# One more pair of projections by seven half products, another order of the projections, and a third row turn laid out by transfers

## The chip, the cores and the metric

The kernel runs on one core of one Trainium2 chip. The metric is the device time of one execution in microseconds (us), median of three runs. The core has a matrix engine (TensorE, PE in the profile; its weight loads are PEld), three engines that work elementwise (VectorE, DVE; ScalarE, ACT; GpSimd, POOL), a queue that issues transfers (SyncE, SP), and 16 DMA engines. Each engine runs its own instructions in order; semaphores tie them together.

## The reference

One encoder layer for 512 tokens of width 1024, all in float32: two attention mixers beside each other (A: windowed, 16 query heads and 4 key heads; B: three groups of four heads with window and dilation (128,1), (512,4), (2048,16)), merged by sigmoid gates, then an output projection, a layer norm, a SwiGLU of width 2816 and a second layer norm.

```python
proj = h @ w_in[l]
qa, ka, va, qb, kb, vb = jnp.split(proj, SPLITS, axis=-1)
qa = rope_partial(qa.reshape(b, s, A_Q_HEADS, HEAD_DIM), pos)
...
o_a = windowed_gqa_sink(qa, ka, va, a_sink[l]).astype(h.dtype)
o_b = dilated_mixture(qb, kb, vb).astype(h.dtype)
gates = jax.nn.sigmoid(h @ w_gate[l] + b_gate[l])
g_a, g_b = jnp.split(gates, N_BRANCH, axis=-1)
mixed = g_a * (o_a @ w_br_a[l]) + g_b * (o_b @ w_br_b[l])
y = mixed @ w_out[l]
h = layer_norm(DN_ALPHA * h + y, ln1_g[l], ln1_b[l])
f = (jax.nn.silu(h @ w_ff_gate[l]) * (h @ w_ff_up[l])) @ w_ff_down[l]
h = layer_norm(DN_ALPHA * h + f, ln2_g[l], ln2_b[l])
```

The rotation (rope) touches the first 16 of the 64 dimensions of a head: it mixes two blocks of eight rows with cosines and sines.

## The kernel before

**Precision.** Every float32 factor is split into a high part (rounded to the engine's fast format, a copy on ScalarE or VectorE, line 387 or 389) and a low part (the rest, a subtraction on VectorE, line 558 or 413). A product is three matmuls: high by high, high by low, low by high.

**Single projections.** 128 output features over 512 tokens are eight blocks of three matmuls of 512 columns (feat_k, lines 537 to 539), 24 matmuls into one bank of PSUM. The weights come as two halves of 256 KB (half_unit), each split once.

**Pairs by seven half products.** pair_x takes two projections at once by the scheme of Strassen and Winograd: a 2 x 2 block product by seven products instead of eight. Each is 12 matmuls of 256 columns (lines 659 to 661). It needs sums of the weight halves: S1 and S3 are loaded with a second transfer that adds in flight (load_sum, issued by POOL at line 401), S2 and S4 are added on VectorE, or for a pair of the kind "D:" by further adding transfers (line 624). All seven factors are split. The token side needs shifted forms of x, made once by x_forms (step X in the order). ScalarE evacuates partial results (keep, line 667), VectorE combines them (lines 680 and 682). A pair holds two banks, y and xz.

**Rotation.** A single q or k is rotated out of its bank (rotate, lines 772 to 778, two VectorE operations that read the bank and two that do not). Results of pairs are rotated in turns of several tiles (turn_rows): transfers gather the 16 rotated rows of each head into one tile G; a second tile H has the same rows with the two blocks of eight exchanged. In the form R, H is made from G by a stream shuffle on VectorE (line 746). In the form r, H is laid out by transfers alone, four more of 16 KB for each tile, straight from the source (line 742). Then follow two products, a sum, and transfers back (line 754).

**Order.** Every operation has a priority: the planned TensorE time T at which its step stands in the list ORDER, plus an offset of the step (the number behind @) and one of its kind (FORMS, EV and others). A greedy planner at build time (Program.run) goes through time with estimated durations, gives each free engine the ready operation of lowest priority whose buffers fit, and so fixes the order of each engine's queue. On the chip every queue is followed in that order. Buffers are slots of SBUF and eight banks of PSUM, handed out first in, first out (b.room, line 274); at most three banks serve the projections (class dense). SPARE slots are kept free for the oldest waiting buffer.

**ORDER's words.** P: and D: are pairs; q, k, Q, K with digits are projections of mixers A and B; VA, V0, V12 are values; g is a gate; A and B are attention units; O fetches an attention output of A from memory (fetch_oa, allowed after the unit that OA_AFTER names); R and r are row turns over everything that waits for one. Two gates are computed along with the first projections k0, q0 and VA; their results and those of the other gates of B are put away in memory and fetched back. Branches (lines 1487 to 1507) multiply the attention outputs by w_br_a and w_br_b and apply the gates; the output projection (tok_major), the norm and the SwiGLU (also by seven half products, lines 1759 to 1761) follow. In ORDER before, 13 pairs stand; the single gates g stand around B2 and behind B3; X stands first; k0 and q0 are rotated right behind the first projections, outside the list (line 1332).

Of the kernel before, what the change touches and what calls it, by code (L numbers as in the profile page):

```python
# [15 lines left out]
P = 128  # L16
S = 512
D = 1024
# [31 lines left out]
SAME = {PE: 0.0, ACT: 0.1, DVE: 0.1, POOL: 0.1}  # L50
HOLD = 0.25
BIAS = 0.2
SPARE, SPARE2 = (4, 12)
ROOMS = {2: dict(whl=16), 3: dict(whl=20, ws=8)}


# [28 lines left out]


ORDER = """
X@-11 VA@-23 q2@-799 q1@-877 P:q3,g@-124 R@-106 D:k1,q4@-31 R@155 P:q5,Q01@-843 A0@-168 D:q6,q7@-47 D:g,g@-34 r@631 P:g,Q00@-22 L@-4 A2@-96
D:g,K00@-31 A1@-48 R@187 V12@-20 P:g,K01@-67 R@-5 P:Q02,K02@-28 A3@-55 V0@55 R@5 B0@-7 B1@11 O@25 O@35 P:K10,Q10@-39 O@-13 O@-54 K11@-34 R@24
O@11 P:Q12,Q11@-30 g@28 K12@-12 O@950 g@25 r O@43 P:g,g@-2 B2@-525 O@-304 B3@21 g@-29 P:g,g@-32 g@-8  # L90
"""
FORMS = -255.0
VAL = 140.0
OA_AFTER = (1, 0, 0, 0, 0, 1, 0, 0)
XT_AFTER, LN_AFTER = [('B', 2), ('B', 2), ('B', 2), ('B', 2)], "b4"
STORE, OA, OA_SPLIT, OB_SPLIT, N_OA, N_XA = 0.0, -60.0, -140.0, -140.0, 4, 4
PACK = -60.0
# [40 lines left out]
class Program:  # L138


    def __init__(self, limits):
        self.limits = limits
        self.used = {k: 0 for k in limits}
        self.ops = []
        self.writer, self.readers = {}, {}
        self.T = 0.0
        self.spare = SPARE
        self.strict = self.hold = False
        self.rooms = {}

    @staticmethod
    def buf_of(tok):
# [2 lines left out]
    def op(self, alts, fn, reads=(), writes=(), prio=0.0, after=(), abs_prio=None, moves=0.0, extra=0, table=None):  # L155
        o = Op()
# [19 lines left out]
        for t in list(reads) + list(writes):  # L176
            b = self.buf_of(t)
# [6 lines left out]
            d.succ.append(o)  # L184
        self.ops.append(o)
        return o

    def fits(self, o):
        need = {}
# [17 lines left out]
    def run(self):  # L207
        engines = (PE, ACT, DVE, POOL, SP)
        free = dict(START)
# [25 lines left out]
        while n_left:  # L235
# [5 lines left out]
            while frees and frees[0][0] <= now:  # L241
                _, _, b = heapq.heappop(frees)
# [6 lines left out]
            while progress:  # L249
                progress = False  # L250
                for e in engines:
# [13 lines left out]
                    o = best  # L265
# [5 lines left out]
                    for b in o.bufs:  # L271
                        if b.tile is None:
                            if b.keys[0] in self.rooms:
                                b.room = self.rooms[b.keys[0]].popleft()
                                b.tile = b.make(b.room)
                            else:
                                b.tile = b.make()
                            for key in b.keys:
                                if key in self.limits:
                                    self.used[key] += 1  # L280
# [64 lines left out]
def hybrid_layer(ctx: ExitStack, tc: tile.TileContext, wpack, xT, xtok, sink, bgate,  # L345
# [20 lines left out]
    def slot(dt=F32, cls=None):  # L366
        cls = cls or "gen"
        return Buf("slot", cls, lambda r: slab.tile([P, S], dt, tag=f"slab{r}", bufs=1, name=name("sl")))

    def bank(cls):  # L370
        return Buf("bank", cls, lambda r: psum.tile([P, S], F32, tag=f"bank{r}", bufs=1, name=name("ps")))
# [85 lines left out]
    def unit(u):  # L457
        return [half_unit(u, 0), half_unit(u, 1)]
# [37 lines left out]
    for j in range(KD):  # L496
# [3 lines left out]
        for c0, c1 in ((0, S // 2), (S // 2, S)) if j == 0 else ((0, S),):  # L500
            w, sk = c1 - c0, (st, c0)
# [45 lines left out]
    def feat_x(ps, wu):  # L547
        for k in range(KD):
            feat_k(ps, wu, k, XM, xtok_of)
# [206 lines left out]
                   reads=gs, writes=[(R, "r", h)], prio=EV)  # L756
            op([(POOL, 0.0)], lambda e: None, reads=[(R, "r", 0), (R, "r", 1)], writes=[R], prio=EV)

    def in_sbuf(u):

        ps, t = bank("dense"), slot()
        feat_x(ps, unit(u))
        op([(ACT, act(S, True))], lambda e: copy(ACT, halves(t.t), back(ps.t)), reads=[ps], writes=[(t, 1), (t, 2)], prio=EV)
        return t

# [551 lines left out]
    psk, psq, psv = bank("dense"), bank("dense"), bank("dense")  # L1317
# [11 lines left out]
    op([(POOL, 0.0)], lambda e: pr.limits.update(whl=N_WHLA, ws=N_WSA), after=[pr.ops[-1]])  # L1329
    for f in range(N_ALONG):  # L1330
        gate(8 + f, ps=along[f])
    ka, qa = {0: k_near(psk, 4)}, {0: q_near(psq, 4, (0, 0))}
    load(mB, maskb, prio=0)
    env = {"gate": N_ALONG, "turn": [], "qs": {}, "ks": {}}

# [57 lines left out]
    def step(w):  # L1393
        if w == "X":
            x_forms()
        elif w == "L":
            op([(POOL, 0.0)], lambda e: pr.limits.update(ws=N_WS, whl=N_WHL), after=[env["mark"]])
        elif w[:2] in ("P:", "D:"):
# [26 lines left out]
        elif w[0] == "A":  # L1425
            g = int(w[1])
# [688 lines left out]
```

## Time and profile before

| | |
|---|---|
| median of three runs | 724.7 us (724.18 to 724.98) |
| the profiled execution | 724.82 us, its span 723.0 us |
| mean granted TensorE clock | 0.998 |
| POOL busy | 173.2 us (24% of the span) |
| instructions | 14810 |
| memory read by transfers | 119.69 MB |
| transfers of 16 KB between tiles (SP) | 28 |
| stream shuffles in row turns (line 746) | 6 |

The span goes from the first to the last instruction on the core; the time of an execution has about 1.8 us around it. Where the prediction shows groups of instructions, each row has the line of the kernel, engine, operation, tiles and shapes, then a count, busy time, the mean ns of one, and the idle time of the engine ahead of them with what ended it. Matmuls overlap: their durations are longer than the distance between their starts.

### The profile page before, as it was taken

How to read it: one execution, taken by the hardware profiler on the slowest of the kernel's cores; microseconds unless marked ns; L12 is line 12 of the kernel's file. 1: busy time of each engine (PE TensorE's matmuls, PEld its weight loads, DVE VectorE, ACT ScalarE, POOL GpSimd, SP SyncE). 2: the span in 40 equal slices, each digit the busy share in tenths (PEclk: the TensorE clock that was granted, in tenths of full speed). 3: DMA queues.
4: the chain of work that ended last, by engine and by line, in shares of the span. 5: the costliest groups of instructions: out<-in, count | busy, mean ns of one | idle time of the engine just before them, and what ended most of it. 6: DMA issues, size and time to landing. Idle time of an engine off the chain costs nothing.

```text
span 723.0 us, 14810 instructions
## 1 busy us (share of the span) xinstructions
PE 712.5 (99%) x4947; PEld 667.2 (92%) x4947; DVE 664.4 (92%) x1425; ACT 494.6 (68%) x1136; POOL 173.2 (24%) x347
## 2 busy tenths in 40 slices
PE   8999999999999999999999999999999999999996
PEld 6889999998999998988888999999999999999985
DVE  6998999999999989999958998999999999999987
ACT  5768889889878997767625666756567566666821
POOL 0113343322423591550020022121121201212000
PEclk9999999999999999999999999999999999999999
DMA  8978967887568789766690499776897868979402
GB/s 257 294 215 210 235 168 213 227 216 179 137 169 204 187 255 253 219 196 219 199 210 33 110 300 232 177 203 165 238 238 197 223 164 219 253 196 194 106 29 88
DMA packets 81275, 141.44 MB, mean 196 GB/s; under 512 B 11024, under 2 KB 15760, under 8 KB 81200
## 3 DMA queue, kind: packets, MB, share of 16 engines
q1 hardware_dynamic: 63472, 107.07, 46.3%
q0 software_dynamic: 17456, 33.30, 26.6%
q8 instruction: 39, 0.64, 0.4%
q14 instruction: 36, 0.29, 0.1%
q10 hardware_dynamic: 272, 0.13, 0.1%
HBM read 119.69 MB, written 8.39 MB: 177 GB/s over the span
## 4 chain that ended last, share of the span: by engine, by line
PE 90%; DMA 4%; DVE 3%; SPq 2%; ACT 1%; issue 0%; POOL 0%; DVEq 0%; ACTq 0%; POOLq 0%
PE ps L1761 10%; PE ps L1759 10%; PE ps L1760 9%; PE ps L659 5%; PE ps L661 5%; PE ps L660 5%; PE ps L537 4%; PE ps L538 4%; PE ps L539 4%; PE ps L1970 4%; PE ps L1972 4%; PE ps L1971 4%; PE ps L1018 3%; DMA sl<-wpack 3%; PE ps L1549 3%; PE ps L1551 3%
## 5 line engine op out<-in xcount | busy, mean ns | idle before, releaser
L387 ACT ACTIVATE sl<-sl 128x512 fp32r<-128x512 f32 (+3 forms) x457 | 253.8, 588 | 60.7 <-DVE sl L558 43.3
L558 DVE TENSOR_TENSOR sl<-sl,sl 128x512 fp32r<-128x512 f32 (+3 forms) x415 | 245.3, 628 | 6.0 <-ACT sl L387 5.0
L387 ACT ACTIVATE sl<-ps 128x256 f32<-128x256 f32 (+6 forms) x214 | 88.5, 440 | 76.6 <-PE ps L1761 53.0
L401 POOL DMA_DIRECT2D sl<-wpack x70 | 63.0, 931 | 319.1 <-DMA sl<-wpack 92.0
L1760 PE MATMUL ps<-sl,sl 128*128 128x256 f32 x352 | 96.8, 275 | 0.0
L1761 PE MATMUL ps<-sl,sl 128*128 128x256 f32 x352 | 96.8, 275 | 0.0
L1759 PE MATMUL ps<-sl,sl 128*128 128x256 f32 x352 | 96.8, 275 | 0.0
L1759 PE MATMUL ps<-x,sl 128*128 128x256 f32 x264 | 72.6, 275 | 0.0
L1760 PE MATMUL ps<-x,sl 128*128 128x256 f32 x264 | 72.6, 275 | 0.0
L1761 PE MATMUL ps<-x,sl 128*128 128x256 f32 x264 | 72.6, 275 | 0.0
L1759 PEld LDWEIGHTS ps<-sl,sl 128*128 128x128 f32 x352 | 67.6, 192 | 0.1
L1760 PEld LDWEIGHTS ps<-sl,sl 128*128 128x128 f32 x352 | 67.6, 192 | 0.1
L1761 PEld LDWEIGHTS ps<-sl,sl 128*128 128x128 f32 x352 | 67.6, 192 | 0.0
L537 PE MATMUL ps<-x,sl 128*128 128x512 f32 (+1 forms) x161 | 62.1, 386 | 0.7 <-ACT x L387 0.7
L539 PE MATMUL ps<-x,sl 128*128 128x512 f32 (+1 forms) x161 | 60.9, 378 | 0.0
L659 PE MATMUL ps<-sl,sl 128*128 128x256 f32 x208 | 57.8, 278 | 0.9 <-ACT sl L667 0.9
L661 PE MATMUL ps<-sl,sl 128*128 128x256 f32 x208 | 57.3, 276 | 0.0
L660 PE MATMUL ps<-sl,sl 128*128 128x256 f32 x208 | 57.2, 275 | 0.0
L558 DVE TENSOR_TENSOR sl<-sl,ps 128x512 f32<-128x512 f32 (+1 forms) x72 | 47.3, 661 | 9.0 <-PE ps L1972 5.8
L1759 PEld LDWEIGHTS ps<-x,sl 128*128 128x128 f32 x264 | 50.6, 192 | 0.4
L1760 PEld LDWEIGHTS ps<-x,sl 128*128 128x128 f32 x264 | 50.6, 192 | 0.4
L1761 PEld LDWEIGHTS ps<-x,sl 128*128 128x128 f32 x264 | 50.7, 192 | 0.0
(174 smaller groups left out, 2006.6 us busy)
## 6 DMA issues: line engine op xcount, KB each, us to landing
sl<-wpack SPq DMA_DIRECT2D x254, 256.0 KB
sl<-wpack POOLq DMA_DIRECT2D x70, 256.0 KB, 5.5
wf<-wpack SPq DMA_DIRECT2D x51, 256.0 KB
sl<-sl SPq DMA_DIRECT2D x56, 128.0 KB
wf<-wpack POOLq DMA_DIRECT2D x24, 256.0 KB, 5.3
oa<-sl POOLq DMA_DIRECT2D x32, 128.0 KB, 3.6
sl<-sl SPq DMA_DIRECT2D x72, 32.0 KB
gz<-sl SPq DMA_DIRECT2D x8, 256.0 KB
```

Of the source, the lines that this page charges most:

```text
L387: nc.scalar.activation(dst, src, AF.Copy)
L401: op([(POOL, 1.0)], lambda e: nc.gpsimd.dma_start(b.t, src2, accum_op=ALU.add), reads=[b], writes=[b], prio=prio, moves=1.65)
L537: mm(o, a, x0, start=(k == 0 and begins), stop=False, skip_group_check=split)
L538: mm(o, a, x1, start=False, stop=False, skip_group_check=split)
L539: mm(o, b, x0, start=False, stop=(k == nk - 1), skip_group_check=split)
L558: op([(DVE, dve(w))], lambda e: nc.vector.tensor_tensor(dst(), x(), y(), op=o), reads=reads, writes=writes, prio=prio)
L659: mm(o, wh, pairs(bh[k]()), start=(first and k == 0), stop=False, skip_group_check=True)
L660: mm(o, wh, pairs(bl[k]()), start=False, stop=False, skip_group_check=True)
L661: mm(o, wl, pairs(bh[k]()), start=False, stop=(k == 3), skip_group_check=True)
L1759: mm(o, wh, pairs(bh[k]()), start=(first and k == 0), stop=False, skip_group_check=True)
L1760: mm(o, wh, pairs(bl[k]()), start=False, stop=False, skip_group_check=True)
L1761: mm(o, wl, pairs(bh[k]()), start=False, stop=(k == 3), skip_group_check=True)
```

## The change

The list ORDER is replaced, with five effects on what runs:

- two single gates become a pair: 14 pairs instead of 13;
- the row turn of Q02 and K02 takes the form r instead of R: three turns of that form instead of two;
- VA and k0 stand ahead of X, q1 ahead of q2, and q0 behind the first row turn; k0 and q0 are now words of the list;
- three pairs of gates stand ahead of B2, and the last single gates stand before B3; B2 and B3 have offsets that put their operations early (-639 and -341 instead of -525 and +21);
- a fetch O stands between B0 and B1, and OA_AFTER lets the first fetch start after B0 instead of B1.

Further, SPARE goes from 4 to 6, FORMS from -255 to -225, and room_for picks banks: a bank of class "d" prefers one whose last user wrote the whole bank.

```diff
-SPARE, SPARE2 = (4, 12)
+SPARE, SPARE2 = (6, 12)
...
 ORDER = """
-X@-11 VA@-23 q2@-799 q1@-877 P:q3,g@-124 R@-106 D:k1,q4@-31 R@155 P:q5,Q01@-843 A0@-168 D:q6,q7@-47 D:g,g@-34 r@631 P:g,Q00@-22 L@-4 A2@-96
-D:g,K00@-31 A1@-48 R@187 V12@-20 P:g,K01@-67 R@-5 P:Q02,K02@-28 A3@-55 V0@55 R@5 B0@-7 B1@11 O@25 O@35 P:K10,Q10@-39 O@-13 O@-54 K11@-34 R@24
-O@11 P:Q12,Q11@-30 g@28 K12@-12 O@950 g@25 r O@43 P:g,g@-2 B2@-525 O@-304 B3@21 g@-29 P:g,g@-32 g@-8
+VA@-29 k0@-34 X@-23 q1@-782 q2@-481 P:q3,g@-83 R@-99 q0@2 D:k1,q4@-37 R@181 P:q5,Q01@-677 A0@-173 D:q6,q7@-58 D:g,g@-53 r@820 P:g,Q00@-13 L@6
+D:g,K00@-4 R@-1 A2@-106 A1@-66 V12@-10 P:g,K01@-81 R@47 P:Q02,K02@-21 V0@48 A3@-45 r@-321 B0@6 O@-29 B1@14 O@-4 O@-99 P:K10,Q10@-39 O@-29
+K11@-33 R@63 O@-6 P:Q12,Q11@-1 O@-11 P:g,g@2 K12@-30 O@10 r@-8 P:g,g@-12 P:g,g@-32 B2@-639 g@12 O@-50 g@6 B3@-341
 """
-FORMS = -255.0
+FORMS = -225.0
 VAL = 140.0
-OA_AFTER = (1, 0, 0, 0, 0, 1, 0, 0)
+OA_AFTER = (0, 0, 0, 0, 0, 1, 0, 0)
...
+    def room_for(self, b):
+        free = self.rooms[b.keys[0]]
+        if b.keys[0] != "bank":
+            return free.popleft()
+        room = next((r for r in free if self.whole.get(r)), free[0]) if b.keys[1] == "d" else free[0]
+        free.remove(room)
+        self.whole[room] = b.keys[1] in ("dense", "o", "d", "dff")
+        return room
...
-                                b.room = self.rooms[b.keys[0]].popleft()
+                                b.room = self.room_for(b)
...
-    ka, qa = {0: k_near(psk, 4)}, {0: q_near(psq, 4, (0, 0))}
+    ka, qa = {}, {}
+    first_of = {"k0": (psk, lambda t, post: ka.update({0: (k_post(t, 4) if post else k_near(t, 4))})),
+                "q0": (psq, lambda t, post: qa.update({0: (q_post(t, 4, (0, 0)) if post else q_near(t, 4, (0, 0)))}))}
...
     def step(w):
         if w == "X":
             x_forms()
+        elif w in first_of:
+            first_of[w][1](first_of[w][0], False)
...
```

In this ORDER only the words k0 and q0 themselves occur, so both go by k_near and q_near as before.

More of the change, by code (lines that the diff above doesn't have):

```diff
@@ L148, in __init__ @@
         self.strict = self.hold = False
-        self.rooms = {}
+        self.rooms, self.whole = {}, {}
     @staticmethod
@@ L757, in turn_rows, with in_sbuf @@
             op([(POOL, 0.0)], lambda e: None, reads=[(R, "r", 0), (R, "r", 1)], writes=[R], prio=EV)
-    def in_sbuf(u):
-        ps, t = bank("dense"), slot()
-        feat_x(ps, unit(u))
+    def in_sbuf(u, ps=None):
+        t = slot()
+        if ps is None:
+            ps = bank("dense")
+            feat_x(ps, unit(u))
         op([(ACT, act(S, True))], lambda e: copy(ACT, halves(t.t), back(ps.t)), reads=[ps], writes=[(t, 1), (t, 2)], prio=EV)
@@ L1395, in step @@
             x_forms()
+        elif w in first_of:
+            first_of[w][1](first_of[w][0], False)
+        elif w[1:] in first_of:
+            first_of[w[1:]][1](first_of[w[1:]][0], True)
+        elif w[2:] in first_of:
+            ps, f = first_of[w[2:]]
+            env["turn"].append((in_sbuf(None, ps), lambda t, f=f: f(t, True)))
         elif w == "L":
```

## The prediction

> **What bounds the kernel now.** I read the page's head and chain, then busy time by stretches, then the waits of TensorE, then its timeline at each wait. The page's busy shares and shares of the chain:
>
> ```profile
> span 723.0 us, 14810 instructions
> ...
> PE 712.5 (99%) x4947; PEld 667.2 (92%) x4947; DVE 664.4 (92%) x1425; ACT 494.6 (68%) x1136; POOL 173.2 (24%) x347
> ...
> PE 90%; DMA 4%; DVE 3%; SPq 2%; ACT 1%; issue 0%; POOL 0%; DVEq 0%; ACTq 0%; POOLq 0%
> ```
>
> The chain that ended last is TensorE for nine tenths of its length. VectorE is the second engine, at 92%. The same by stretches (columns: PE, PEld, DVE, ACT, POOL busy with counts, granted clock, DMA share, GB/s):
>
> ```profile
> 260.00:300.00 40.00, 39.60 (x242) 35.57 (x241) 36.25 (x96) 29.35 (x76) 16.30 (x42) 1.00 0.94 243
> 300.00:340.00 40.00, 40.00 (x225) 35.98 (x224) 37.25 (x103) 28.67 (x74) 16.51 (x63) 1.00 0.65 210
> ...
> 412.00:716.00 304.00, 303.97 (x2281) 290.90 (x2278) 286.05 (x547) 185.35 (x399) 52.03 (x60) 1.00 0.74 190
> 716.00:723.00 7.00, 0.00 (x0) 0.00 (x0) 3.93 (x8) 0.29 (x1) 0.00 (x0) 0.84 0.30 112
> ```
>
> TensorE is full wherever the change does not reach: from 412 to 716 us it idles 0.03 us, and the 7 us behind it are the last normalisation and its store, which the change leaves alone. So the time moves by two things only: matmul work taken out, and stalls that come or go before 412 us. All stalls of TensorE that the view of waits names:
>
> ```profile
> PE ps L473 <- DVE eps L524: 1.2, 1, 1.2
> PE ps L659 <- ACT sl L667: 0.9, 1, 0.9
> PE ps L537 <- ACT x L387: 0.7, 1, 0.7
> PE ps L1018 <- ACT sl L1006: 0.4, 1, 0.4
> ```
>
> The first and third are the kernel's start, before any reordered step. Only 0.9 + 0.4 us are left to win from waits. That makes a big gain impossible, whatever the new order does.
>
> **The change part by part.** *The fourteenth pair.* Two gates leave the single form and become a pair. A single gate is 24 matmuls of 512 columns, two are 48; a pair is seven products of 12 matmuls of 256 columns, 84. What one costs is the distance from start to start, since the durations overlap:
>
> ```profile
> 6.59 0.38 PE L537 MATMUL ps<-x,sl 128*128 128x512 f32 x1
> ...
> 36.80 0.38 PE L539 MATMUL ps<-x,sl 128*128 128x512 f32 x1
> 37.02 0.27 PE L659 MATMUL ps<-x,sl 128*128 128x256 f32 x1
> ...
> 39.59 0.28 PE L661 MATMUL ps<-x,sl 128*128 128x256 f32 x1
> ```
>
> The first two rows are 141 matmuls, 140 steps: 30.21 / 140 = 0.2158 us. The last two are 24, 23 steps: 2.57 / 23 = 0.1117 us. So 48 x 0.2158 = 10.36 us become 84 x 0.1117 = 9.38 us: **-0.98 us**, on an engine without slack, so it counts in full. Bounds: nothing, if a stall fills it, and -0.98.
>
> A rule speaks against this. The Trainium skill, "Perfetto Trace Analysis", section Identifying the Most-Contended Engine, says matmul busy time misleads and weight-load busy time shows how loaded TensorE is.
>
> ```profile
> 340.00:350.00 10.00, 10.00 (x49) 8.74 (x48) 9.99 (x18) 4.83 (x9) 0.00 (x0) 1.00 0.51 168
> ...
> 420.00:460.00 40.00, 40.00 (x361) 40.00 (x360) 37.23 (x75) 25.80 (x56) 8.80 (x11) 1.00 0.94 249
> ```
>
> At 340 us, almost all 512 columns, a matmul brings 8.74 / 48 = 0.182 us of load busy time; at 420 us, mostly 256 columns, 40.00 / 360 = 0.111. If loads set the pace, 48 x 0.182 = 8.74 would become 84 x 0.111 = 9.33, +0.59 us in place of -0.98. By that rule the exchange loses. I go by start-to-start, because 512-column matmuls follow each other at 0.2158 us while their loads leave 13% of the time free; the rule stays as a rival.
>
> *What the pair adds elsewhere.* The rows of the engines that feed TensorE (mean ns of one):
>
> ```profile
> L558 DVE TENSOR_TENSOR sl<-sl,sl 128x512 fp32r<-128x512 f32 x261 | 173.8, 684 | 5.4 <-ACT sl L387 5.0
> L558 DVE TENSOR_TENSOR sl<-sl,ps 128x512 f32<-128x512 f32 x66 | 44.9, 683 | 9.0 <-PE ps L1972 5.8 <-PE ps L1761 2.3 <-PE ps L661 0.4
> L682 DVE SCALAR_TENSOR_TENSOR sl<-ps,sl 128x256 f32<-128x256 f32 x13 | 5.4, 418 | 0.3 <-PE ps L904 0.2
> L746 DVE STREAM_SHUFFLE sl<-sl 64x512 f32<-64x512 f32 x3 | 2.2, 732 | 0.0
> L387 ACT ACTIVATE sl<-sl 128x512 fp32r<-128x512 f32 x378 | 225.1, 623 | 55.1 <-DVE sl L558 41.8 <-PE ps L538 2.7 <-DMA sl<-oa 2.2
> L667 ACT ACTIVATE sl<-ps 128x256 f32<-128x256 f32 x52 | 19.4, 376 | 4.5 <-PE ps L661 4.3
> ```
>
> VectorE: seven low parts instead of four (3 x 0.684), two sums of weights (2 x 0.684), one sum with the bank (0.683), one combination (0.418): 4.5 us. ScalarE: three high parts more (3 x 0.623) and four evacuations (4 x 0.376): 3.4 us, where it idles 22 of 80 us (260 to 340: 58.0 busy). VectorE idles 80 - 73.5 = 6.5 us there, so the 4.5 us fit, but leave it 97% busy; that is the cover, and with it gone each microsecond too many is TensorE's, up to +4.5. I take 0, the row's free time being larger.
>
> *Transfers of the pair.* Five loads and two sums in flight, issued by POOL, instead of four loads:
>
> ```profile
> q1 hardware_dynamic: 63472, 107.07, 46.3%
> q0 software_dynamic: 17456, 33.30, 26.6%
> ...
> sl<-sl SPq DMA_DIRECT2D x28, 16.0 KB
> ...
> L401 POOL DMA_DIRECT2D sl<-wpack x70: 848/865/1782, 23.9 to 650.9; - x70
> ...
> L732 SPq DMA_DIRECT2D sl<-sl x36: 507/551/1559, 47.2 to 252.7; - x36
> ...
> DMA to landing us min/median/max: 3.8/5.5/10.3
> ```
>
> SP's queue gets one more load, POOL's two more issues (2 x 0.865 us). A megabyte takes 0.463 x 723 / 107.07 = 3.1 us of the 16 engines by q1, 5.8 by q0; with 0.262 MB a piece that is 0.8 + 2 x 1.5 = 3.8 us. From 260 to 300 us the engines are free 2.4 us, from 300 to 340 us 14 us. Value 0, since loads run far ahead of use; upper bound a late sum, priced below.
>
> *The third row turn by transfers.* Of the eight turns, that of Q02 and K02 changes form. It loses one shuffle of 64 rows, 0.73 us of VectorE, and gains eight transfers of 16 KB, each about 0.55 us of SP's queue (row L732): 4.4 us in which later weight loads stand behind them. VectorE's net addition is thus 4.5 - 0.7 = 3.8 us. Value 0; bounds -0.7 and, if a weight load is needed just then, +4.4.
>
> *The start.* The shifted forms of x (step X) now come after the turned values VA and k0; q0's rotation moves behind the first row turn. Today's wait there:
>
> ```profile
> 41.07 0.64 ACT L387 ACTIVATE sl<-sl 128x512 fp32r<-128x512 f32 x1 [1.55 <-DVE sl L558]
> ...
> 41.98 1.15 ACT L387 ACTIVATE sl<-sl 128x512 fp32r<-128x512 f32 x2 [0.28 <-ACT sl L387]
> ...
> 42.27 0.28 PE L661 MATMUL ps<-sl,sl 128*128 128x256 f32 x1
> ...
> 43.04 0.64 ACT L667 ACTIVATE sl<-ps 128x256 f32<-128x256 f32 x2
> ...
> 43.46 0.38 PE L659 MATMUL ps<-sl,sl 128*128 128x256 f32 x1 [0.91 <-ACT sl L667]
> ```
>
> Start to start is 1.19 us here, so the stall is 1.19 - 0.11 = 1.08. ScalarE evacuated the bank (L667) only behind three copies into high parts, and those had waited 1.55 us for VectorE. Moving q0 takes four 512-wide VectorE operations and two low parts (6 x 0.684 as at L558 = 4.1 us) out of the stretch ahead: the stall may go, -1.08. Against it, q0's bank stays taken. Three banks serve this work; with one held, the pair's second bank waits until q2's has been read (two operations, 1.4 us, and one queued ahead, 0.7) with one product (12 x 0.1117 = 1.34) as cover: +0.75. I take **-0.3**, a little below the middle (-0.17), since the measured wait is the nearer row.
>
> *Fetches of attention outputs, B2 and B3 early, gates ahead.* One late chain is there:
>
> ```profile
> 261.01 6.40 DMA sl<-oa
> 267.43 3.51 DMA sl<-sl
> ...
> 278.92 0.41 ACT sl L1006
> 279.38 0.89 PE ps L1018 x5
> ```
>
> A fetch now allowed one unit earlier can end this 0.4 us wait or crowd other transfers in the fullest stretch: -0.4 to +0.4, taken as 0. "All gates ahead" moves little on TensorE, which today leaves the gates (their moving operand is x) before the first branch:
>
> ```profile
> 300.65 0.38 PE L539 MATMUL ps<-x,sl 128*128 128x512 f32 x1
> 300.87 0.38 PE L537 MATMUL ps<-sl,sl 128*128 128x512 f32 x1
> ```
>
> *Two slots more in reserve and another choice among free banks:* no instruction added; 0, bounds 0 to one evacuation (0.7).
>
> **Sum.** -0.98 - 0.3 = -1.28 us, so the profiled span becomes 721.7. The profiled execution took 724.8 us, 1.8 around its span, against a median of 724.7: **723.4 us**. About 0.2% (1.45 us) is what a measurement of this kernel can tell from no change; the bound of faster is 723.25, so the forecast lies just inside no change.
>
> **The rivals.**
> 1. *Given back within the noise.* VectorE at 97% from 260 to 340 us, or q0's held bank, returns 1 to 2 us (half of 3.8 us is 1.9). For: at 97% an operation that comes late is not caught up soon. Against: TensorE waits only 0.4 us there today, with VectorE 92% busy. Around 725.0.
> 2. *More is won.* Both waits go: -0.98 - 1.08 - 0.4 = -2.5, 722.2. For: both have a cause that the order touches. Against: the held bank.
> 3. *Slower: the sums in POOL's queue.* In the run of gate pairs each pair needs two sums, and POOL issues in order, behind unit B's cross copies (POOL 16.3 us busy from 260 to 300) and the output fetches. A sum that lands at 10.3 instead of 5.5 us is 4.8 late; the two products before its first use cover 2.7 only if nothing was ahead of schedule. One uncovered sum: -0.98 + 4.8 = +3.8, 728.5; covered, +1.1. It is slower by the bound from 2.4 us uncovered; middle 727. The issue of such a sum took 0.865 us in the median and 1.782 at most (row L401). The Trainium skill, "SBUF — State Buffer", section SBUF: two separate sides, warns that copies on VectorE can lock POOL out and stretch an issue of 0.62 us to 3.1; nothing in this trace reaches that. Against: no TensorE wait on a weight's DMA stands in the view today, with 26 such sums.
> 4. *Loads set the pace.* +0.59 (and -0.3): 725.0.
> 5. *It does not do what it says.* The gates already stand ahead of the branches; then only the pair's 0.98 remains: 723.7, inside the forecast.
>
> **How the numbers follow.** Forecast (722.7 to 724.2, rival 5 in it) 0.54; rival 1, 0.20; rival 2, 0.11; rival 3, 0.13; rival 4, 0.02. Faster: rival 2 and half of the forecast, since 723.25 nearly halves it, 0.11 + 0.27 = 0.38. Same: the other half, rivals 1 and 4, 0.49. Slower 0.13. The range reaches from the full gain, 722.0, to where rival 3 begins, 726.4.
>
> **What would show it.** Right: 84 more L659 to L661 matmuls and 48 fewer with x at L537 to L539, steps of 0.1117 us, last matmul 1 to 2.5 us earlier, tail 7 us. L746 with five shuffles instead of six, and 36 instead of 28 transfers of 16 KB. Wrong: a TensorE wait over 1 us, above all on a split (L387 or L558) between 260 and 340 us or on L774 or L772 near 40 us; POOL's landing above 5.5 us beside such a wait; a tail or a feed-forward stretch that changes length.

## The result and the profile after

The changed kernel takes 729.3 us (median of 4 runs, 728.04 to 729.76) against 724.5 us (724.18 to 724.98) for the kernel before in the same runs: a ratio of 1.0063, interval 1.0051 to 1.0075. It is slower by 0.6%, and the forecast of 723.4 us, with its range up to 726.4, is missed. The profiled execution took 728.95 us, its span is 726.9 us. (Of two experiments below, single_again and hoist, the profiled execution was a disturbed one and is left out; single_look and hoist_look are second runs of them.)

The head, chain and transfer queues of the page after:

```profile
span 726.9 us, 14912 instructions
...
PE 713.5 (98%) x4983; PEld 667.8 (92%) x4983; DVE 666.8 (92%) x1428; ACT 498.4 (69%) x1145; POOL 174.9 (24%) x349
...
q1 hardware_dynamic: 63744, 107.46, 46.6%
q0 software_dynamic: 17744, 33.83, 27.1%
...
PE 87%; DMA 5%; DVE 3%; SPq 2%; POOL 1%; issue 1%; ACT 1%; DVEq 0%; POOLq 0%; ACTq 0%
```

TensorE's share of the chain fell from 90 to 87%, that of transfers rose from 4 to 5%. Where TensorE waits now (engine, line waited for; us in total, times, longest):

```profile
PE ps L1220 <- DVE sl L1054: 1.7, 1, 1.7
PE ps L482 <- DVE eps L533: 1.2, 1, 1.2
PE ps L668 <- ACT sl L676: 0.6, 1, 0.6
PE ps L547 <- DVE sl L1370: 0.5, 1, 0.5
```

The wait of the start (L668 behind L676) shrank from 0.9 to 0.6 us. New at the top is a wait of 1.7 us in attention unit B (L1220). By stretches (PE, PEld, DVE, ACT, POOL busy, granted clock, DMA share, GB/s):

```profile
260.00:300.00 40.00, 38.02 (x245) 34.00 (x244) 35.38 (x94) 30.66 (x80) 14.64 (x42) 1.00 1.05 270
300.00:340.00 40.00, 39.53 (x227) 35.45 (x226) 36.28 (x101) 27.77 (x74) 21.28 (x67) 1.00 0.64 201
412.00:718.00 306.00, 306.00 (x2299) 292.96 (x2297) 288.48 (x551) 185.95 (x401) 53.76 (x62) 1.00 0.74 191
718.00:726.90 8.90, 0.02 (x1) 0.00 (x0) 3.93 (x8) 0.29 (x1) 0.00 (x0) 0.71 0.25 90
```

Three things are to be seen against the rows of before. Between 260 and 300 us TensorE loses 1.98 us instead of 0.40, VectorE is busy for less time (35.38 instead of 36.25 us), and the DMA engines are full (1.05, before 0.94). The stretch from 412 us to the last matmul is untouched. And behind the last matmul the span goes on for 8.9 us, not 7.1.

**The accounts.** Start to start, each matmul has a regular distance (0.2158 us for 512 columns, 0.1117 for 256). What the distances exceed it, summed over the trace, is TensorE's lost time: 7.6 us before, 10.6 us after. The last matmul ends at 715.97 us before and at 718.02 after: +2.05 = 3.03 of lost time - 0.98 of the pair. Of the 3.03, 2.80 lie between 260 and 340 us (1.67 before, 4.47 after), 0.28 from 240 to 260, 0.28 from 60 to 200, 0.33 from 340 to 360; the first 60 us won 0.66. The rest of the span's 3.9 us is the tail, 7.07 against 8.87: +1.80.

**The wait in unit B.** VectorE's timeline ahead of it:

```profile
273.31 0.69 DVE L422 TENSOR_TENSOR sl<-sl,sl 128x512 fp32r<-128x512 f32 x1 [1.84 <-ACT sl L396]
273.92 0.69 DVE L1370 TENSOR_TENSOR sl<-sl,sl 128x512 fp32r<-128x512 f32 x1
274.52 0.68 DVE L1034 TENSOR_TENSOR sl<-ps,sl 128x512 fp32r<-128x512 f32 x1
276.02 0.43 DVE L398 CAST sl<-sl 128x512 fp32r<-128x512 f32 x1 [0.81 <-DMA sl<-wpack]
276.48 0.69 DVE L422 TENSOR_TENSOR sl<-sl,sl 128x512 fp32r<-128x512 f32 x1
277.09 0.68 DVE L1370 TENSOR_TENSOR sl<-sl,sl 128x512 fp32r<-128x512 f32 x1
277.69 0.75 DVE L1054 TENSOR_TENSOR sl<-ps,sl 128x256 fp32r<-128x256 f32 x2
```

TensorE's own rows there:

```profile
276.05 0.38 PE L548 MATMUL ps<-x,sl 128*128 128x512 f32 x1
278.16 0.88 PE L1220 MATMUL ps<-sl,sl 128*128 128x256 f32 x4 [1.74 <-DVE sl L1054]
```

The chain of the window from 255 to 320 us:

```profile
266.67 9.32 DMA sl<-wpack
276.02 0.44 DVE sl L398
...
278.16 0.88 PE ps L1220 x4
...
290.83 8.32 DMA sl<-oa
299.19 0.47 issue
299.66 0.86 POOL sl L1385
```

Read from the end: TensorE waits for two low parts of unit B (L1054). They stand in VectorE's queue behind the split of a weight half (L398, L422) and of an O block (L1370). That weight was issued by SP at 266.67 us and landed 9.3 us later. VectorE has nothing to do with these weights that is urgent; it goes in order and stands still: 1.84 us for a copy of ScalarE, which was itself released by a landing at 272.56 and the end of a matmul at 272.62 us, and 0.81 us for the load. The last rows are a second case: POOL waits for an O block that lands after 8.3 us, adds its second part (L1385), and only then comes to unit B's small copies, which stand behind it in its queue; VectorE waits for these, and at 312.1 us TensorE waits 0.5 us (L547).

### The profile page after: what moved, and what is told of

The parts are those of the page before. It is cut to its first block, busy times and chain, and to the rows that moved or that the text cites. A ratio compares the mean times of both kernels' runs of the same rounds, so it can differ in the third digit from the quotient of the medians.

```text
span 726.9 us, 14912 instructions
## 1 busy us (share of the span) xinstructions
PE 713.5 (98%) x4983; PEld 667.8 (92%) x4983; DVE 666.8 (92%) x1428; ACT 498.4 (69%) x1145; POOL 174.9 (24%) x349
## 4 chain that ended last, share of the span: by engine, by line
PE 87%; DMA 5%; DVE 3%; SPq 2%; POOL 1%; issue 1%; ACT 1%; DVEq 0%; POOLq 0%; ACTq 0%
PE ps L1780 9%; PE ps L1781 9%; PE ps L1779 9%; PE ps L668 6%; PE ps L670 6%; PE ps L669 6%; PE ps L1990 4%; PE ps L1992 4%; PE ps L1991 4%; PE ps L547 3%; PE ps L548 3%; PE ps L546 3%; PE ps L1029 3%; PE ps L1570 3%; PE ps L1571 3%; PE ps L1569 3%
## 5 line engine op out<-in xcount | busy, mean ns | idle before, releaser
L567 DVE TENSOR_TENSOR sl<-sl,sl 128x512 fp32r<-128x512 f32 (+3 forms) x424 | 250.7, 628 | 4.2 <-ACT sl L396 3.4
L396 ACT ACTIVATE sl<-ps 128x256 f32<-128x256 f32 (+5 forms) x208 | 85.7, 436 | 72.7 <-PE ps L1781 52.3
L1780 PE MATMUL ps<-sl,sl 128*128 128x256 f32 x352 | 96.8, 275 | 0.0
L1781 PE MATMUL ps<-sl,sl 128*128 128x256 f32 x352 | 96.8, 275 | 0.0
L1779 PE MATMUL ps<-sl,sl 128*128 128x256 f32 x352 | 96.8, 275 | 0.0
L668 PE MATMUL ps<-sl,sl 128*128 128x256 f32 x224 | 62.5, 279 | 0.6 <-ACT sl L676 0.6
L669 PE MATMUL ps<-sl,sl 128*128 128x256 f32 x224 | 61.6, 275 | 0.0
L670 PE MATMUL ps<-sl,sl 128*128 128x256 f32 x224 | 61.6, 275 | 0.0
L546 PE MATMUL ps<-x,sl 128*128 128x512 f32 (+1 forms) x145 | 56.0, 386 | 0.0
L548 PE MATMUL ps<-x,sl 128*128 128x512 f32 (+1 forms) x145 | 54.7, 378 | 0.0
```

Source lines behind the costliest of these rows:

```text
L396: nc.scalar.activation(dst, src, AF.Copy)
L546: mm(o, a, x0, start=(k == 0 and begins), stop=False, skip_group_check=split)
L548: mm(o, b, x0, start=False, stop=(k == nk - 1), skip_group_check=split)
L567: op([(DVE, dve(w))], lambda e: nc.vector.tensor_tensor(dst(), x(), y(), op=o), reads=reads, writes=writes, prio=prio)
L668: mm(o, wh, pairs(bh[k]()), start=(first and k == 0), stop=False, skip_group_check=True)
L669: mm(o, wh, pairs(bl[k]()), start=False, stop=False, skip_group_check=True)
```

## The experiments

The theory: the 16 DMA engines are full from 260 to 300 us because of the pair's transfers, loads land late, and VectorE's queue, which holds their splits in order, passes the delay on to TensorE. Its rivals: VectorE is short of capacity; the cause is another part of the change; the order in SP's queue, not the bytes.

All ratios are to the kernel before on the same chip. The last matmul, the lost time from 260 to 340 us and the tail are read from one profiled execution of each kernel.

| kernel | median us | ratio, interval | last matmul | lost 260 to 340 | tail |
|---|---|---|---|---|---|
| before | 724.5 | | 715.97 | 1.67 | 7.1 |
| after | 729.3 | 1.0063 (1.0051 to 1.0075) | 718.02 | 4.47 | 8.9 |
| unblock | 728.0 | 1.0049 (1.0036 to 1.0061) | 717.45 | 3.26 | 8.2 |
| no_pair_sums | 725.8 | 1.0019 (1.0010 to 1.0028) | 715.42 | 2.10 | 8.1 |
| no_oa_sums | 725.1 | 1.0008 (0.9999 to 1.0017) | 714.85 | 0.86 | 8.0 |
| before_more | 727.4 | 1.0045 (1.0033 to 1.0057) | 717.69 | 2.74 | 7.5 |
| hoist (trace: hoist_look) | 727.1 | 1.0035 (1.0022 to 1.0048) | 717.22 | 3.50 | 7.7 |
| pad | 728.1 | 1.0053 (1.0040 to 1.0065) | 718.24 | 4.61 | 8.0 |
| last_sem | 727.6 | 1.0055 (1.0042 to 1.0067) | 717.02 | 2.90 | 8.1 |
| best | 726.5 | 1.0032 (1.0020 to 1.0044) | 716.53 | 2.73 | 7.0 |
| early | 731.5 | 1.0090 (1.0076 to 1.0104) | 722.80 | 5.46 | 7.1 |
| single_look | 727.5 | 1.0041 (1.0026 to 1.0056) | 716.51 | 0.59 | 8.8 |

### One word of the order changed, all planned anew

The first four kernels change one thing in the source and let the planner fix the queues again. In single_again, turn_R and pair_only a part of the residual that some blocks preload into their bank is left out of the result (where it is lost, no run here shows); the instructions are the same.

```diff
 single_again: the changed kernel with
-r@-8 P:g,g@-12 P:g,g@-32 B2@-639
+r@-8 g@-12 g@-12 P:g,g@-32 B2@-639
 fetch_back: the changed kernel with
-B0@6 O@-29 B1@14 O@-4
+B0@6 B1@14 O@-29 O@-4
-OA_AFTER = (0, 0, 0, 0, 0, 1, 0, 0)
+OA_AFTER = (1, 0, 0, 0, 0, 1, 0, 0)
 turn_R: the changed kernel with
-A3@-45 r@-321 B0@6
+A3@-45 R@-321 B0@6
 pair_only: the kernel before with
-B3@21 g@-29 P:g,g@-32 g@-8
+B3@21 P:g,g@-29 P:g,g@-32
```

single_again: 

> The changed kernel with one of its three pairs of gates ahead of B2 made two single gates again, all else as changed (the planner orders anew). Theory 1, the pair's own transfers overfill the DMA engines between 250 and 300 us (share 1.01, 1.08, 1.04, 1.08 in the changed kernel, 0.92, 1.04, 1.05, 0.74 before): the share falls below 1 in at least two of these four stretches, the 1.7 us wait of TensorE near 276 us goes, and the time falls from 729.3 to about 725.5, in spite of 0.98 us more of matmuls. Rival, the fetches of attention outputs one unit earlier do it: the wait stays, 729 to 730.5. Of the tail behind the last matmul (8.9 us changed, 7.1 before) neither says anything.

fetch_back: 

> The changed kernel with the fetch O back behind B1 and allowed only after B1, as before; the pair stays. Theory 1 (the pair's transfers overfill the DMA engines): the waits between 260 and 320 us stay near 3 us in sum, 728.5 to 730. Rival (the early fetches do it): the DMA share between 250 and 280 us falls, the wait near 276 us goes, 725.5 to 726.5.

turn_R: 

> The changed kernel with the row turn of Q02 and K02 by the shuffle again. It takes out 8 transfers of 16 KB near 200 to 230 us and adds 0.73 us to VectorE. Theories 1 and 2 alike: no effect by itself on the stretch behind 250 us, so 728 to 730, apart from what the new order brings. Rival, the small transfers delay SP's queue for what follows: 725.5 to 727.

pair_only: 

> The kernel before with one edit: its last two single gates become a pair, behind B3 where they stood. If the pair itself costs (its transfers, or VectorE's 4.5 us more), the time rises to 726 or more, with waits between 260 and 320 us. If it only saves its matmuls, 723.5, with the waits as before.

None of the four decided anything. single_again took 729.4 us (1.0058, interval 1.0041 to 1.0075), a time that its rival gave, but without a trace that shows the wait. The others took 735.7, 738.3 and 739.9 us, outside of what any theory gave or, for pair_only, far above it. Their largest waits are not the ones under test. Of fetch_back:

```profile
PE ps L546 <- ACT sl L396: 4.9, 1, 4.9
```

Of pair_only:

```profile
PE ps L537 <- ACT sl L387: 5.0, 1, 5.0
```

Five microseconds at the start of the branches, which neither the kernel before nor the changed one has. One word in the list moves thousands of instructions, so undoing a word measures the planner's next order, not the word. The kernel of single_again once more, as single_look, for its trace:

> The changed kernel planned anew with two single gates instead of its fourteenth pair (the residual that some blocks preload is lost in part of them), for its trace. If the pair's transfers are the whole story, the DMA share of 260 to 300 us is under 1.0 in two of the four windows and PE's waits of 260 to 340 us sum to 2.5 us or less, and what keeps it at 729.4 us is PE's work (0.98 us more than with the pair), a tail of 8 us or more, and waits elsewhere. If other parts of the change fill the engines as well (the O blocks fetched a unit earlier, the row turns by transfers), the share is 1.0 or more in three of them and the waits are 4 us or more without the pair.

Its busy time and its first wait:

```profile
260.00:300.00 40.00, 40.00 (x244) 36.48 (x243) 35.62 (x94) 29.73 (x79) 18.12 (x49) 1.00 1.03 258
```

```profile
PE ps L1650 <- DVE sl L1632: 1.4, 2, 0.8
```

Without the pair TensorE loses nothing between 260 and 300 us. What keeps this order slow lies elsewhere: 2.98 us lost from 380 to 460 us (0.71 in the changed kernel) and a tail of 8.8 us, of a kind of its own: the last store goes out 6.3 us after the last matmul, in the kernels before and after 4.6. Its DMA share is 1.03 all the same: full engines cost nothing by themselves here, only a transfer that lands after its use does. My expectation had the share fall below 1.0 in two of four windows; it did in one (0.96).

From here on the plan is frozen: the kernel plans as before, keeps the list of operations with their queues (log), edits that list by hand, and only then writes the instructions. How much the lost time differs from execution to execution is seen in three profiles of this order with no edit near 260 to 340 us: 4.47 (after), 4.61 (pad) and 2.90 us (last_sem). In these kernels lines are numbered 15 higher (L1235 for L1220, L683 for L668).

### VectorE's queue: unblock

```diff
+late = [log[nth(log, DVE, n)] for n in (507, 508, 509)]
+to = log[nth(log, DVE, 514)]
...
+log = [o for o in log if o not in late]
+b = log.index(to) + 1
+log[b:b] = late
```

> The order of every instruction of the changed kernel is kept as it was planned; only three of VectorE's are moved: the high copy and the two low parts that wait for a weight load and an O block (lines 398, 422 and 1370 of the trace at 276.02 to 277.09) go behind the four low parts of unit B's turned scores (line 1054, 277.69 to 278.80). Theory (a load that lands late blocks VectorE's queue in front of work that PE waits for): PE's wait of 1.74 us in front of line 1220 at 278.16 falls under 0.3 us, nothing else gets longer, and the time falls from 729.3 to about 727.6 (727.2 to 728.0). Rival (VectorE is short of capacity there, or PE is late for the same weights a few matmuls on): the wait moves to a neighbour and the time stays within 0.4 us of 729.3.

728.0 us. The one wait of 1.74 us became two, and another came at line 1278:

```profile
PE ps L1235 <- DVE sl L1069: 0.7, 2, 0.4
PE ps L1278 <- DVE sl L990: 0.7, 1, 0.7
```

VectorE's copy behind which the wait stood is gone, yet the low parts now wait for ScalarE (2.19 us at 276.97), which had stood 1.09 us for a late half at 272.22 and was busy from there on. So the path through VectorE's queue is what the trace showed and VectorE had capacity, but the gain falls short: 1.7 us were expected, the medians show 1.3 and the last matmul of the profiles 0.57 (1.2 less lost from 260 to 340 us, 0.3 more from 240 to 260, the rest at the start); another 0.70 is a shorter tail. The intervals of the two ratios overlap, and 3.26 us lost lies inside the spread of the three profiles above, so that the gain in time is not shown. Two queues held the late loads, and only one was moved.

### Bytes out: no_pair_sums and no_oa_sums

```diff
+gone = {id(log[nth(log, POOL, n)][0]) for n in (138, 139)}
+log = [o for o in log if id(o[0]) not in gone]
```

> The order of every instruction of the changed kernel is kept; only the two transfers of POOL's queue at 254.27 and 255.04 us that add W22 to W21 and W21 to W11 for the fourteenth pair are left out, so that this pair's two half products use the first addend alone. Theory P (the pair's extra transfers are what fills the 16 DMA engines): the weight load that is issued at 266.67 and took 9.3 us lands at least 1.5 us sooner, PE's wait before line 1220 falls under 0.5 us, time 727.6 or less. Rival Q (these sums have landed by 261.6 us, before the engines are full, so that the later transfers are what matters): the load lands within 1 us of 275.99, the wait stays over 1.2 us and the time stays within 0.4 us of 729.3.

This kernel leaves out the second addend of two of the pair's factors:

```profile
260.00:300.00 40.00, 39.10 (x254) 35.54 (x253) 37.51 (x101) 32.07 (x85) 18.78 (x52) 1.00 1.05 263
```

The last matmul ends 2.60 us earlier than in the changed kernel, and 725.8 us are measured; by the ratios, 1.0063 and 1.0019, the difference is 3.2 us, 0.8 of it tail in the profiles. VectorE's copy of the late weight starts at 274.08 us and no longer waits for its transfer. Rival Q falls although its observation was correct: the sums have landed by 261.6 us, but what follows them in the queues starts as much later. The four O sums went out at 259.5 to 262.6 us here, at 263.2 to 265.6 in the changed kernel. Ahead of them POOL is idle in both kernels and waits for the O loads, so that it is their landing that moved and not POOL's queue (changed kernel, then this one):

```profile
263.22 3.53 POOL L1385 DMA_DIRECT2D sl<-oa  x4 [7.22 <-DMA sl<-oa]
...
259.50 2.62 POOL L1400 DMA_DIRECT2D sl<-oa  x3 [5.38 <-DMA sl<-oa]
```

The share stays at 1.05: it shows that the engines are full, not how long the queue before them is.

no_oa_sums has the numbers 140 to 143 in the same edit.

> The order of every instruction of the changed kernel is kept; only the four transfers of POOL's queue at 263.22 to 266.74 us, which add the second part of four O blocks of attention output A, are left out, so that these blocks hold their first part alone. Theory D (the 16 DMA engines are full from 260 to 300 us, and whatever is taken out of there comes back as shorter landings): the weight load issued at 266.67 lands 3 us sooner or more, SP's issues of 1.3 to 1.9 us at 266.67 to 271.76 go back to about 0.5, the waits of 1.84 and 0.81 us in VectorE's queue and PE's wait of 1.74 us go, time 727.5 or less, about 727.3. Rival (the load is late for another reason, such as the order in which SP's queue is served): it lands within 1 us of 275.99 and the time stays within 0.4 us of 729.3.

```profile
260.00:300.00 40.00, 39.90 (x264) 36.73 (x263) 38.61 (x103) 33.10 (x88) 14.58 (x40) 1.00 0.99 264
```

TensorE's lost time from 260 to 340 us falls to 0.86 us, below that of before, and the last matmul ends at 714.85 us, 1.12 before the kernel before: the pair's gain is there as soon as the loads come in time. (This kernel leaves out four sums that the kernel before has too, so it shows the gain in a relieved stretch, not a kernel of equal work.) The time is still 725.1, for the tail is 8.0.

### The same bytes added to the kernel before: before_more

```diff
+for to, o in ((b, (MORE[0], SP)), (a, (MORE[1], POOL)), (c, (MORE[2], POOL))):
+    log.insert(log.index(to), o)
```

MORE are a load of 256 KB and two sums of 256 KB into a tile that nothing reads.

> The kernel before, its order kept, with one more weight load (issued at about 250 us) and two more sums of 128x512 on POOL's queue (at about 254 and 258 us) into a tile that nothing reads: as many transfers as the fourteenth pair adds, without anything else of the change. Theory P (the pair's transfers alone fill the DMA engines of this stretch): the DMA share of 260 to 300 us rises to 1.0 or more in three of the four windows, PE's waits of 260 to 340 us rise from 1.67 to 2.5 us or more, and last matmul's end comes 0.8 to 2.8 us later. The one load more also moves the last store's semaphore from the eighth to the first: the tail behind the last matmul grows from 7.1 to about 8.0 us by the theory of the checks. Time 726.2 to 728.2, about 727. Rival (this order has room for the bytes): waits and last matmul as before, time 724.5 to 725.6 by the tail alone.

727.4 us, in the range. Its windows:

```profile
250.00:260.00 10.00, 9.79 (x88) 9.60 (x86) 6.65 (x14) 8.68 (x27) 8.23 (x25) 1.00 1.04 259
260.00:270.00 10.00, 9.12 (x66) 8.49 (x67) 9.67 (x22) 8.67 (x22) 9.18 (x26) 1.00 0.94 296
...
280.00:290.00 10.00, 8.84 (x56) 7.84 (x55) 9.23 (x23) 8.11 (x23) 1.72 (x2) 1.00 1.06 271
```

The last matmul ends 1.72 us later than before with not one matmul, copy or split more. (About 1.0 us of it is a wait that starts at 259.8 and so lies outside the column of 260 to 340.) The engines fill ten microseconds earlier than I wrote (1.04 from 250 to 260 us); the share of 260 to 300 is not higher than before. And the path is another one than in the changed kernel:

```profile
254.25 0.86 POOL L479 DMA_DIRECT2D more<-wpack  x1 [0.99 <-DMA more<-wpack]
...
259.06 0.17 DVE L1186 TENSOR_TENSOR st<-st 128x8 f32<-128x8 f32 x1 [2.77 <-POOL st L1179]
...
260.60 0.38 PE L674 MATMUL ps<-sl,sl 128*128 128x256 f32 x1 [0.80 <-ACT sl L682]
```

POOL waits for the load to land before it can add to it, and unit B's small copies stand behind in its queue. VectorE waits 2.77 us for them (1.32 before, at 257.93), ScalarE for VectorE, TensorE for ScalarE. The later wait (1.2 us at line 1033, 0.4 before) is for an O sum that POOL starts 2.2 us later than before (269.89 in place of 267.69 us) and that lands no slower (7.5 and 7.6 us). So, as far as the waits show, the added transfers cost TensorE 1.7 us here through the time that they hold POOL's queue; that the bytes alone would do it is not shown by this kernel. With no_pair_sums, where the landings moved, both sides give the pair's transfers a cost of 1.7 to 2.6 us, more than its matmuls save.

### The order in the queue: hoist and early

```diff
+o3, w2, w3 = (log[nth(log, SP, n)] for n in (282, 317, 318))
+bring(291, o3)
+bring(293, o3)
+bring(321, w2)
```

bring puts a load, with the reservation of its slot, ahead of another in SP's queue.

> The order of the changed kernel is kept; only three loads are brought forward in SP's queue, with nothing left out: the two weight loads issued at 265.08 and 266.67 us go ahead of the last two of the four O loads at 258.82, and the last O load of 290.83 goes ahead of the weight loads of 287.94. Theory (the engines are full, and the order in the queue decides what is late; these weights are needed at 273 to 276, the O blocks later): VectorE's waits of 1.84 and 0.81 us at 273 and 276 go, PE's wait of 1.74 us before line 1220 falls under 0.5 us, the waits after 290 us shrink or stay, and the time falls by 1.2 to 2.5 us to about 727.2. Rival (with the engines full for 40 us, what is put behind is late in its place): PE's waits between 260 and 340 us sum to 4 us or more as before (4.47) and the time stays within 0.5 us of 729.3.

The same kernel once more, as hoist_look, for its trace:

> The kernel hoist again, for its trace; time near 727.1. If the three loads brought forward remove the wait: none over 0.5 us between 260 and 300 us, the sum of 260 to 340 us at 2.0 us or less. If they move it: one wait of 1.0 us or more at another line before 300 us, as at 271.5 us (line 683 behind line 706 of VectorE) with the three edits together, and a sum of 2.5 to 3.5 us in place of 4.47.

```profile
PE ps L683 <- DVE sl L706: 2.3, 1, 2.3
...
270.88 0.32 DVE L413 CAST sl<-sl 128x256 fp32r<-128x256 f32 x1 [2.53 <-DMA sl<-sl]
```

727.1 and 727.0 us, as expected in the time, but not for the reason: the wait of 1.74 us before unit B went, and one of 2.3 us came from 271.8 us on in front of a pair's product. VectorE had stood 2.53 us ahead of it for a transfer between tiles that now goes out later: what was put back in the full queue is late in its place. Lost from 260 to 340 us are 3.50 in place of 4.47, which lies inside the spread of the three profiles.

early adds to best (below) the five loads of the gates ahead of eight row transfers:

```diff
+for load, to in zip(late5, (r0, r0, r0, r3, r5)):
+    bring([x for x in log if x[1] == SP].index(load) + 1, to)
+push(138, 137)
+push(139, 138)
```

> The three edits together (best), and with them the five weight loads of the fourteenth pair and the gate units beside it issued ahead of eight row transfers in SP's queue (about 245 us in place of 249.5 to 252.8) and the pair's two sums ahead of eight of POOL's small copies (about 252 in place of 254.3). If what counts is when the bytes start, the DMA share of 240 to 250 us rises from 0.62 to 0.75 or more, that of 260 to 300 us falls, PE's waits of 260 to 340 us fall from 2.7 to 1.7 us or less, and the time goes to 725.5 or less (best: 726.5). If the transfers passed over are needed as soon, new waits come between 245 and 270 us and the time is 726.5 or more.

731.5 us: the second case. The share of 240 to 250 us did rise, to 0.87, but the row transfers that were passed over were needed at once. VectorE stood 3.74 us for one of them, ScalarE for VectorE and TensorE for ScalarE (the last two rows show matmuls at half their pace, of which more at the end):

```profile
257.12 0.69 DVE L773 TENSOR_TENSOR sl<-sl,sl 96x512 f32<-96x512 f32 x1 [3.74 <-DMA sl<-sl]
...
259.62 0.38 PE L683 MATMUL ps<-sl,sl 128*128 128x256 f32 x1 [3.71 <-ACT sl L691]
...
260.66 0.42 PE L683 MATMUL ps<-sl,sl 128*128 128x256 f32 x1
260.87 0.42 PE L684 MATMUL ps<-sl,sl 128*128 128x256 f32 x1
```

### The tail: pad, last_sem and best

```diff
 pad
+at = log.index(log[nth(log, DVE, 692)])
+log[at:at] = [(PAD[0], DVE)] * 40
 last_sem
+at = log.index(log[nth(log, DVE, 692)])
+log[at:at] = [(p, SP) for p in TINY]
```

pad: 

> The order of every instruction of the changed kernel is kept; 40 memsets of 128x1 are put into VectorE's queue where it is idle (372 to 382 us), which moves every later instruction of VectorE 40 places on in its program. Theory (the 8192-byte fetch of instructions at 723.54 us is VectorE's next 128 instructions, and the last store's packets stand behind it on one DMA engine): no such fetch lies between 721 and 725 us, the last store lands 1.1 to 1.3 us after its issue ends in place of 1.98, and the time falls by 0.7 to 0.9 us to about 728.5. Rival (the fetch is another engine's, or the store is late for another reason): the landing stays near 2 us and the time within 0.3 us of 729.3.

last_sem: 

> The order of the changed kernel is kept; seven loads of 128x1 are put into SP's queue at about 380 us, so that the eight semaphores of SP's transfers, which are dealt in turn, give the last store the eighth instead of the first. Theory (the program's end checks these semaphores in their order, so that after the last store's landing seven more checks of 62 ns and a gap of 0.37 us follow when it has the first): the last store's check becomes the last of the ten, the drain follows it within 0.1 us, and the time from the last store's landing to the span's end falls from 2.3 us to 1.4 to 1.6; time down by 0.7 to 0.9 us, to about 728.5. Rival (the end takes as long whatever is checked last): within 0.3 us of 729.3.

Both edits and hoist together:

> The three edits together that leave nothing out: the three loads brought forward, the seven small loads that shift the last store's semaphore, and VectorE's 40 small memsets that move its instruction fetch out of the end. If the three causes are separate and add up (about 2.1, 0.8 and up to 0.9 us of 729.3): 725.5 us, 724.8 to 726.5, still not below the kernel before (724.5). If the full DMA engines only move the waits: 727.5 or more.

Transfers between the last store's issue and its landing, after (queue: packets, MB, share of 16 engines):

```profile
q1 hardware_dynamic: 346, 0.35, 49.4%
q14 instruction: 1, 0.01, 1.4%
```

and in best:

```profile
q1 hardware_dynamic: 347, 0.35, 83.2%
```

The same store takes 1.98 us with one instruction fetch in that interval and 1.12 us without. Read from each trace's transfers and semaphore events (us):

```text
kernel       last matmul  last store issued  landed         its check         tenth check  span's end
before       715.97       720.57             721.70 (1.13)  tenth, 722.14     722.14       723.04
after        718.02       722.64             724.62 (1.98)  third, 725.11     725.57       726.89
pad          718.24       722.85             723.98 (1.13)  third, 724.40     724.87       726.19
last_sem     717.02       721.63             723.63 (2.00)  tenth, 724.20     724.20       725.11
best         716.53       721.14             722.26 (1.12)  tenth, 722.67     722.67       723.57
before_more  717.69       722.29             723.43 (1.14)  third, 723.85     724.27       725.16
```

Two causes, separate. From issue to landing pad takes 0.85 us away: the fetch is VectorE's, since only VectorE's program was moved. From landing to end it takes 2.27 us after and 1.48 in last_sem, where the last store's semaphore is checked last; before_more shows the same from the other side, 1.34 to 1.73 us. Seven checks are 0.46 us of this (725.11 to 725.57); the rest of last_sem's 0.79 us is a pause of 0.34 us behind the changed kernel's tenth check, which before_more does not have. best has both and the tail of before, 7.0 us. Of the medians pad (728.1) and last_sem (727.6) alone little can be said, because the loss between 260 and 340 us differs from execution to execution: 4.61 us in the one profile, 2.90 in the other, with no edit near it.

best takes 726.5 us, 725.39 to 728.45 in six runs: a microsecond more than the sum of the three terms. The profiled execution is the fastest of them, 725.39 us, and still has the wait that hoist moves (1.67 us, from 271.9 us on); what the slower ones lose is not known. No version tried is below the kernel before.

## Why the prediction was wrong

**The pair's matmuls, -0.98: right.** The page's counts after, and those of before behind them:

```profile
L668 PE MATMUL ps<-sl,sl 128*128 128x256 f32 x224 | 62.5, 279 | 0.6 <-ACT sl L676 0.6
...
L546 PE MATMUL ps<-x,sl 128*128 128x512 f32 x143 | 54.9, 384 | 0.0
...
L668 PE MATMUL ps<-x,sl 128*128 128x256 f32 x168 | 46.8, 279 | 0.0
```

```profile
L537 PE MATMUL ps<-x,sl 128*128 128x512 f32 x159 | 61.3, 385 | 0.0
...
L659 PE MATMUL ps<-sl,sl 128*128 128x256 f32 x208 | 57.8, 278 | 0.9 <-ACT sl L667 0.9
...
L659 PE MATMUL ps<-x,sl 128*128 128x256 f32 x156 | 43.3, 277 | 0.0
```

16 + 12 matmuls of 256 columns more at each of three lines, 16 of 512 columns fewer: 84 and 48. The last matmul of no_oa_sums shows the gain itself. Weight-load busy time did grow by 0.6 us (667.2 to 667.8), as rival 4 had it, but the time does not follow it. The Trainium skill, "Perfetto Trace Analysis", section Identifying the Most-Contended Engine, names weight-load busy time, beside the share of peak that the matmuls reach, as the way to judge TensorE's headroom; read as a price it would make the exchange lose 0.59 us, and the start-to-start distances of these traces decide against that.

**The start, -0.3: right in this profile,** 1.08 to 0.73 us. But profiles of the same order show 0.45 to 1.08 us there (pad 0.51, last_sem 1.08), so that a single profile neither confirms nor refutes a term of this size.

**VectorE as cover: right.** Over the whole span it is busy 2.4 us more (664.4 to 666.8), not 3.8. It was less busy than before where TensorE waited, and in no_oa_sums it did the same work in time. Rival 1 had the wrong engine.

**The pair's transfers, "Value 0, since loads run far ahead of use": the step that failed.** The prediction had both numbers side by side, 3.8 us of DMA time and 2.4 us free from 260 to 300 us, and no row behind "far ahead". In the changed kernel a weight half issued at 266.67 us landed 9.3 us later, and VectorE already stood waiting for it. Measured: 1.7 us (before_more) to 2.6 us (no_pair_sums) instead of 0. The rivals allowed for a late sum as rival 3, and there the stretch was right, the carrier half: the long wait came through plain loads of SP and VectorE's queue. POOL's queue carried the short wait at 312.1 us and the first one of before_more, but the other way round than rival 3 had it: not a sum stood behind unit B's small copies, the copies stood behind a sum. (Two details of rival 3's working: the landing times of 3.8, 5.5 and 10.3 us are those of the sums of row L401, though they are printed below row L732. And by its own condition it begins at 724.7 + 1.45 = 726.15 us, not 726.4.)

**The tail, "which the change leaves alone": failed too,** by 1.80 us. The work in it is unchanged (last matmul to VectorE's end 4.07 us in both). What changed is where in VectorE's program its next fetch of 8192 bytes falls (0.85 us of landing), and which of the semaphores the last store got (0.46 us of checks and a pause of 0.34 in the other 0.93): the number of instructions and of transfers ahead, nothing in the tail itself.

**Left open.** What the fetch of O one unit earlier costs (taken as 0, bounds 0.4) and what the third row turn costs (0, bounds -0.7 to +4.4) was not separated: with a new plan the answer is drowned. So the earlier O fetch may have its share in the full stretch of 260 to 300 us. The O sums lie in the full stretch and weigh 3.2 us there (no_oa_sums), but the kernel before has them too; early shows only that row transfers have no slack. 0.9 us of lost time outside of 260 to 340 us was not traced. SPARE, FORMS and room_for were not tried alone.

## What to carry to other kernels

A change that trades matmul time for bytes is to be priced in the stretch where the bytes pass, not at the average: where 2.4 us of the DMA engines were free and 3.8 were added, the matrix engine paid 1.7 to 2.6 us, through whichever in-order queue held the work behind a late landing. A full stretch alone says nothing (single_look lost nothing in one); ask which load has no time to spare. What transfers cost is best tested with the plan frozen: take out two, or add two that nobody reads. Then look at the path as well, since an added transfer also holds the queue that issues it. An unchanged tail can still change, by a fetch of instructions in front of the last store and by the order in which semaphores are checked at the end.

## What the hardware showed unexpectedly

- An instruction fetch on one DMA engine ahead of the last store's packets delayed its landing from 1.13 to 1.98 us; 15 of 16 engines had finished 0.87 us earlier. It comes and goes with little: unblock, with 1857 recorded instructions on VectorE instead of 1858, has no fetch at that place, and its store landed in 1.11 us.
- With full DMA engines three of SP's issues of single transfers in a row took 1.59, 1.94 and 1.33 us (266.67 to 271.76 us after); those just ahead took 0.46 to 0.50 us.
- After TensorE's stop of 3.71 us in early, matmuls of 256 columns followed at 0.21 us in place of 0.11 from 260.2 to 263.4 us. The Trainium skill, "TensorE: Matmul & The Clock Gate", section What's actually happening, says that the clock falls to half after an idle window of about 3.4 us and returns after as long a busy one; the trace agrees, with a stop of 3.7 us, a granted clock of 0.60 from 259.6 to 262 us and 0.62 from 262 to 264, and full speed 3.8 us after the stop's end (259.62 to 263.43).
- Each check of a passed semaphore at the end of SP's program took about 0.06 us, 0.46 us for the seven behind the last store's.
